# A float32 transformer trunk on one core: another opening, and four seven-product chunks in the last stage

## The chip, the core and the metric

The kernel runs on one core of one Trainium2 chip. The metric is the device time of one execution in microseconds (us). The engines named below: TensorE (PE in the profile; PEld is its weight load), VectorE (DVE), ScalarE (ACT), GpSimd (POOL) and SyncE (SP), which issues most DMAs. Each engine works through its own instructions in program order; an instruction whose operands are not ready holds everything behind it on that engine.

## What is computed

Two layers of a streaming encoder on 256 frames of width 1024, all in float32. Each layer is a half-step SwiGLU network (hidden width 2816), attention (chunked with a relative bias in layer 0, differential with rotary in layer 1, both beside a cross-attention into a memory of 256 rows), and a second half-step SwiGLU network:

```python
for i in range(DEPTH):
    h = rmsnorm(x, ffn1_norm[i])
    x = x + 0.5 * swiglu(h, ffn1_w_gate[i], ffn1_w_up[i], ffn1_w_down[i])
    h = rmsnorm(x, mix_norm[i])
    proj = h @ w_in[i]
    ...
    x = x + jnp.concatenate([o_s, o_m], axis=-1) @ w_out[i]
    h = rmsnorm(x, ffn2_norm[i])
    x = x + 0.5 * swiglu(h, ffn2_w_gate[i], ffn2_w_up[i], ffn2_w_down[i])

def swiglu(h, w_gate, w_up, w_down):
    return (jax.nn.silu(h @ w_gate) * (h @ w_up)) @ w_down
```

The row scale of `rmsnorm` is applied behind the product, so the gate and up products start from x times the gain, before the mean square is known.

## The kernel before

**Split products.** A float32 operand is split into a high part that TensorE's fast float32 mode (`F32R`) holds exactly, and a low part, the rest. A product of a weight tile and an x tile is then three matmuls into one PSUM bank: high times high, low weight times high x, high weight times low x. `dense` (L504) issues them, at L511, L514 and L517. Weights arrive in chunks of 1 MB (128 partitions by 2048 columns, `raw`); ScalarE casts the high parts (`split_hi`, L338), VectorE subtracts the low parts (`split_lo`, L356), both in pieces. Three raw buffers and four pairs of high and low buffers go round. `Item.units` lists the pieces that a chunk is split into.

**Gate and up.** A network has 11 groups of 256 hidden columns. A group's gate and up columns lie side by side, 512 columns. K is 1024, eight tiles of 128, so a group has two chunks, `c` = 0 for K tiles 0 to 3 and `c` = 1 for 4 to 7. For each of the two token blocks (`tb`, 128 frames each) a group accumulates in one PSUM bank; `plain_chunk` (L750) runs `dense` over token blocks and tiles, 24 matmuls for a chunk. `evac` (L624) applies the row scale and the activation behind a group, turns the result (`h`, `hb`) and sends it through DRAM (`hd`, `hr`) to become the operand of the down product. In each network, two of the groups are done as seven products instead of eight (`pair_forms`, `product`); for these VectorE forms four sums of the x tiles (L780) and their splits (`xf`, L784 and L787) as soon as all of x is there.

**Down.** 11 chunks of 256 rows by 1024 columns, each eight products of three matmuls; chunks listed in `SEVEN` take seven products (`seven`, `seven_item`): VectorE forms four sums of the weight tiles (L350, `wsum`), seven pieces are split rather than four, and the operand gets sums of its own (`seven_forms`, L681 and L694). The first chunk of the list takes two buffer pairs; the others are guests: their last pieces lie in the tiles that hold x's split parts at other times (`xt_room`), one guest at a time. Chunks 8 to 10 run at the end, one output quarter after the other (`SPLIT`), and `finish` adds each quarter to x.

**Order.** The program is written out by hand-set rules: a planner (`Flow`) keeps a clock of its own while the code is being generated. PE's work advances it (0.216 us for a matmul); each helper is a thread (a Python generator) that yields the time or the condition at which its next step is due, and steps are put into the engines' programs when the planner's clock reaches them. Threads go ahead of idle threads; the loader and the two splitters are idle threads. A splitter also waits until its engine is nearly free (`calm_a`, `calm_v`), and the pair forms wait for VectorE to be nearly free in the same manner.

**The opening.** `load_x` (L185) loads x in quarters (token block by half of the columns); the first half of each block is issued at the start, on SP's and ScalarE's queues. The loader issues the first chunk in eight pieces, the second in four, with the second half of block 0 behind the first chunk and that of block 1 in the middle of the second. A small array of gains is transposed (L1631); PE runs warm products of the identity, four at the start, then two and five (L1646, called from L1636 and L1638). `start` (L1640) prepares the quarters of x at the planner's times 3.4, 8.8, 5.6 and 10.8: `prep_half` (L547) transposes four tiles on PE (L525), scales them by the gain on VectorE (`y`, L557), casts the high part on ScalarE (`xh`, L560) and subtracts the low part on VectorE (`xl`, L562). Then the first network goes through group 0's two chunks, in halves of two K tiles, for both token blocks.

Of the kernel before, what the change touches and what calls it, by code (L numbers as in the profile page):

```python
# [142 lines left out]
def kernel(  # L143
# [40 lines left out]

    def load_x(tb, hf, queue=None):  # L185
        (queue or nc.sync).dma_start(out=xs[tb][:, hf * 512:(hf + 1) * 512],
                                     in_=x[0, tb * P:(tb + 1) * P, hf * 512:(hf + 1) * 512])

    load_x(0, 0)
    load_x(1, 0, nc.scalar)  # L190

# [55 lines left out]
    class Item:  # L247
# [3 lines left out]
        def __init__(self, raws, uses=8, w=1):  # L251
            self.raws, self.uses = raws, uses
            self.hi = self.lo = None
            self.hit, self.lot, self.st = [None] * 7, [None] * 7, [None] * 4
            self.n, self.frees, self.takes, self.gives, self.guest = 1, 1, 0, 0, False
            self.sums, self.t = [], []
            self.index = len(items)
            w = 1 if len(items) < 2 else w
            self.units = [(self.own(q, w), q, w, None) for q in range(0, 4, w)]
            items.append(self)  # L260
# [13 lines left out]
    xt_room = [False]  # L274
    dma_free = [2.5]
    LAT = 1.5
# [9 lines left out]
    def loader():  # L286
        for i, c in enumerate(chunks):
            yield lambda: raw_left[0] > 0
            raw_left[0] -= 1
            c.raw = wraw.tile([P, 2048], F32, tag="raw", name=f"raw{i}")  # L290
            dma_free[0] = max(dma_free[0], flow.now)
            n = len(c.parts)
            for j, (dst, src) in enumerate(c.parts):
                nc.sync.dma_start(out=dst(c.raw), in_=src)
                dma_free[0] += 2.9 / n
                if i < 2 and j % 2:
                    for q in range((j - 1) * 4 // n, (j + 1) * 4 // n):
                        c.block[q] = dma_free[0] + LAT
                if i == 1 and j == 1:
                    load_x(1, 1)  # L300
                    dma_free[0] += 0.7
            c.arrive = dma_free[0] + LAT
            c.block = [t or c.arrive for t in c.block]
            if i == 0:
                load_x(0, 1)
                dma_free[0] += 0.7
            if i > 4 and late_done[0] < len(late_loads):
                dst, src = late_loads[late_done[0]]
                late_done[0] += 1
                nc.sync.dma_start(out=dst, in_=src)  # L310
                dma_free[0] += 0.3
# [30 lines left out]
    def split_lo():  # L342
        for i, it in enumerate(items):
# [8 lines left out]
            for src, q, w, dep in it.units:  # L352
                yield lambda: it.hit[q] is not None
                yield it.hit[q]
                yield calm_v(i)
                nc.vector.tensor_sub(it.part(1, q, w), src(), it.part(0, q, w).bitcast(F32))  # L356
                t = flow.dve(512 * w)
                it.lot[q:q + w] = [t] * w
            raw_left[0] += it.frees
            g2.give(it.gives)  # L360
# [15 lines left out]

    SEVEN = {(0, 1): (), (0, 2): (1, 4, 7), (1, 1): (1, 4, 7), (1, 2): (1, 4, 7)}
    PAIR = {(0, 1): 4, (0, 2): 3, (1, 1): 3, (1, 2): 3}
# [63 lines left out]
    def plan_ffn(l, nm, wg, wu, wd):  # L442
# [7 lines left out]
        pair = PAIR[l, nm]  # L450
        work = [(g, c) for g in range(NG) for c in range(2)]
        if pair is not None:
            rest = [w for w in work if w[0] not in (pair, pair + 1)]
# [50 lines left out]
    def dense(ps, xh, xl, ready, c, need, start, stop):  # L504
# [17 lines left out]
        return flow.pe(T_MM)  # L522

    def turn(dst, src, flipped=False):
        nc.tensor.transpose(out=dst, in_=src, identity=flip if flipped else ident)  # L525
        return flow.pe(T_TR)
# [9 lines left out]
    class Xt:  # L536
        def __init__(self, keep=False):
# [6 lines left out]
            self.done = [0, 0]  # L544
            self.keep, self.y, self.ft = keep, {}, [None] * 4

    def prep_half(xt, tb, hf, gc, wait=0.0):  # L547
# [10 lines left out]
        banks.give()  # L558
        yield flow.dve(512)
        nc.scalar.copy(out=xt.h[tb][:, ks, :], in_=y)  # L560
        yield flow.act(512)
        nc.vector.tensor_sub(xt.l[tb][:, ks, :], y, xt.h[tb].bitcast(F32)[:, ks, :])  # L562
        if xt.keep:
            xt.y[tb, hf] = y
        else:
            g2.give()
# [51 lines left out]
    def ffn(l, nm, xt, gc_next):  # L618
# [230 lines left out]
        if (l, nm) != (0, 1):  # L849
            for tb in range(2):  # L850
                for c in range(2):
                    plain_chunk(0, c, (tb,))
        else:
            for c in range(2):
                for ks in ((0, 1), (2, 3)):
                    plain_chunk(0, c, range(2), ks)
        work = work[2:]
        for w in work:
# [770 lines left out]
    def start_gain():  # L1629
        tp = bank("gps0")  # L1630
        nc.tensor.transpose(out=tp[:, 0, :16], in_=g1row, identity=ident[:16, :16])  # L1631
        yield flow.pe(T_TR)
        nc.vector.tensor_copy(gcol[:, 0:16], tp[:, 0, :16])
        banks.give()
        flow.dve(16)
        warm(2)  # L1636
        yield 4.6
        warm(5)  # L1638

# [10 lines left out]
    warm(4)  # L1650
    table_hint(AF.Silu)
    flow.now = 2.7
    flow.spawn(start_gain())
    for tb in range(2):
        for hf in range(2):
            flow.spawn(start(tb, hf, (3.4, 8.8, 5.6, 10.8)[2 * tb + hf]))
    flow.spawn(gain_columns())
# [61 lines left out]
```

## Time and profile before

| | |
|---|---|
| Time, median of 3 runs | 954.87 us (954.74 to 955.77) |
| The profiled execution: its own time | 955.69 us |
| Its span, from first to last instruction | 953.9 us |
| DVE busy | 820.0 us (86%) |
| ACT busy | 587.0 us (62%) |
| Bytes moved by DMA | 204.04 MB, 214 GB/s on the mean |
| Share of the chain that ended last: PE, DVE, DMA, ACT | 90%, 6%, 2%, 1% |

A line of the timeline gives the start, the time taken, the engine, the line of the kernel, the operation, output and inputs by name, and the count where several are merged; in brackets, how long the engine had been idle and what ended that. A line of the groups gives busy time, mean of one in ns, and idle time ahead of it. A line of the windows gives, for a stretch, the busy time of PE, PEld, DVE, ACT and POOL, the granted clock, the share of the DMA engines and GB/s.

### The profile page before, as it was taken

What the parts mean: (1) busy time and instruction counts of PE and PEld (TensorE: products, weight loads), DVE (VectorE), ACT (ScalarE), POOL (GpSimd) and SP (SyncE); (2) the same over time, 40 slices, a digit from 0 to 9 for tenths busy, and PEclk for the clock granted to TensorE, in tenths of its full rate; (3) what the DMA queues carried; (4) which work ended last, traced back from release to release, by engine and by line L of the source; (5) the groups of instructions that cost most, each with busy time, mean ns of one, the idle gap of its engine ahead of it and who ended that gap; (6) DMA issues with size and microseconds to landing.
All of it is one profiled execution on the core that took longest, in us unless ns stands there. A gap on an engine that the chain in (4) does not pass through costs nothing.

```text
span 953.9 us, 13334 instructions
## 1 busy us (share of the span) xinstructions
PE 945.6 (99%) x4475; PEld 774.1 (81%) x4475; DVE 820.0 (86%) x1483; ACT 587.0 (62%) x1121; POOL 109.1 (11%) x160
## 2 busy tenths in 40 slices
PE   9999999999999999999999999999999999999998
PEld 7888888887777888888888888888787778888886
DVE  7898978888777899979889899796999888999884
ACT  6556566677676746647546656564676865665650
POOL 1000057621210100000000000000434200000000
PEclk9999999999999999999999999999999999999999
DMA  8987799486525387887746679775641367588751
GB/s 265 289 263 236 224 354 296 158 276 210 177 90 177 97 266 225 262 287 219 245 146 219 208 226 288 247 253 166 196 158 57 121 214 228 183 275 276 239 197 45
DMA packets 169887, 204.04 MB, mean 214 GB/s; under 512 B 10137, under 2 KB 145114, under 8 KB 169818
## 3 DMA queue, kind: packets, MB, share of 16 engines
q1 hardware_dynamic: 169498, 202.78, 66.0%
q8 instruction: 35, 0.57, 0.3%
q10 hardware_dynamic: 320, 0.40, 0.1%
q14 instruction: 34, 0.28, 0.1%
HBM read 188.99 MB, written 14.16 MB: 213 GB/s over the span
## 4 chain that ended last, share of the span: by engine, by line
PE 90%; DVE 6%; DMA 2%; ACT 1%; issue 1%; SPq 0%; ACTq 0%; DVEq 0%
PE gu L517 13%; PE gu L514 13%; PE gu L511 13%; PE acc L511 9%; PE acc L517 9%; PE acc L514 9%; PE pair_m L511 3%; PE pair_m L514 3%; PE pair_m L517 3%; PE pj L517 2%; PE pj L511 2%; PE pj L514 2%; DVE lo L356 2%; PE S L1360 1%; DMA x<-in_x_dram 1%; PE AV L1441 1%
## 5 line engine op out<-in xcount | busy, mean ns | idle before, releaser
L338 ACT CAST hi<-raw 128x512 fp32r<-128x512 f32 (+1 forms) x467 | 336.3, 770 | 172.6 <-DMA raw<-in_ffn_w_up_dram 45.6
L356 DVE TENSOR_TENSOR lo<-raw,hi 128x512 fp32r<-128x512 f32 (+1 forms) x467 | 391.9, 875 | 35.5 <-ACT hi L338 35.4
L514 PE MATMUL gu<-lo,xh 128*128 128x512 f32 x576 | 224.7, 390 | 0.5 <-DVE lo L356 0.5
L517 PE MATMUL gu<-hi,xl 128*128 128x512 f32 x576 | 224.5, 390 | 0.4 <-DVE xl L562 0.4
L511 PE MATMUL gu<-hi,xh 128*128 128x512 f32 x576 | 224.4, 390 | 0.0
L517 PEld LDWEIGHTS gu<-hi,xl 128*128 128x128 f32 x576 | 108.1, 188 | 23.9 <-DVE xl L562 1.7
L514 PEld LDWEIGHTS gu<-lo,xh 128*128 128x128 f32 x576 | 108.1, 188 | 23.5 <-DVE lo L356 1.4
L511 PEld LDWEIGHTS gu<-hi,xh 128*128 128x128 f32 x576 | 108.2, 188 | 22.3
L517 PE MATMUL acc<-hi,ht 128*128 128x512 f32 x280 | 109.5, 391 | 0.0
L511 PE MATMUL acc<-hi,ht 128*128 128x512 f32 x280 | 109.2, 390 | 0.0
L514 PE MATMUL acc<-lo,ht 128*128 128x512 f32 x280 | 109.1, 390 | 0.0
L338 ACT CAST hi<-wsum 128x512 fp32r<-128x512 f32 x82 | 47.7, 619 | 26.5 <-DVE wsum L350 26.5
L514 PE MATMUL pj<-lo,xh 128*128 128x512 f32 x160 | 64.0, 400 | 0.0
L517 PE MATMUL pj<-hi,xl 128*128 128x512 f32 x160 | 63.8, 399 | 0.0
L511 PE MATMUL pj<-hi,xh 128*128 128x512 f32 x160 | 63.8, 399 | 0.0
L514 PEld LDWEIGHTS acc<-lo,ht 128*128 128x128 f32 x280 | 52.6, 188 | 10.9
L517 PEld LDWEIGHTS acc<-hi,ht 128*128 128x128 f32 x280 | 52.6, 188 | 10.8
L511 PEld LDWEIGHTS acc<-hi,ht 128*128 128x128 f32 x280 | 52.6, 188 | 10.7
L532 POOL TENSOR_TENSOR xr<-v,nhalf 128x1 f32<-128x1 f32 x12 | 10.3, 861 | 435.1 <-DVE v L530 435.1
L356 DVE TENSOR_TENSOR lo<-wsum,hi 128x512 fp32r<-128x512 f32 x82 | 52.8, 680 | 0.0
L633 ACT ACTIVATE sil<-gu,xr 128x256 f32<-128x256 f32 x72 | 33.7, 468 | 29.8 <-PE gu L517 29.7
L532 POOL TENSOR_TENSOR hf<-v,nhalf 128x8 f32<-128x8 f32 (+1 forms) x20 | 31.4, 1570 | 87.3 <-DVE v L530 78.9
(232 smaller groups left out, 1429.5 us busy)
## 6 DMA issues: line engine op xcount, KB each, us to landing
raw<-in_ffn_w_down_dram SPq DMA_DIRECT2D x176, 256.0 KB, 4.5
raw<-in_ffn_w_gate_dram SPq DMA_DIRECT2D x82, 512.0 KB, 4.0
raw<-in_ffn_w_up_dram SPq DMA_DIRECT2D x82, 512.0 KB, 5.4
raw<-in_w_in_dram SPq DMA_DIRECT2D x32, 512.0 KB, 4.4
hd<-hb SPq DMA_DIRECT2D x44, 256.0 KB, 4.6
hr<-hd SPq DMA_DIRECT2D x44, 256.0 KB, 4.6
raw<-in_w_out_dram SPq DMA_DIRECT2D x8, 1024.0 KB, 5.1
raw<-in_w_mem_kv_dram SPq DMA_DIRECT2D x4, 1024.0 KB, 5.3
```

What stands on the lines that cost most here:

```text
L338: nc.scalar.copy(out=it.part(0, q, w), in_=src())
L356: nc.vector.tensor_sub(it.part(1, q, w), src(), it.part(0, q, w).bitcast(F32))
L511: nc.tensor.matmul(out=ps, lhsT=xh, rhs=wh, start=start, stop=False)
L514: nc.tensor.matmul(out=ps, lhsT=xh, rhs=wl, start=False, stop=False)
L517: nc.tensor.matmul(out=ps, lhsT=xl, rhs=wh, start=False, stop=stop)
L532: nc.gpsimd.tensor_tensor(out=dst, in0=v[:, :n], in1=nhalf[:, :n], op=ALU.pow)
L633: nc.scalar.activation(sil, ps[tb][:, 0:256], AF.Silu, scale=xt.r[tb])
L1360: nc.tensor.matmul(out=ss[e][:, pr, :nk], lhsT=q[rows, pr, :], rhs=k[rows, pr, :], start=i == 0, stop=i == len(passes) - 1)
L1441: nc.tensor.matmul(out=av[64 * e:64 * e + 64, pr, :], lhsT=vsrc(kb, pr, e), rhs=pts[e][:, pr, kb, :], start=(kb == 0), stop=(kb == nb - 1))
```

## The change

Four things are changed.

1. x comes in other pieces. Block 0's first half is loaded in two pieces on two queues; block 1's first half is issued behind the first two weight pieces; the second halves come behind the second chunk. Three of the first chunk's eight pieces go through ScalarE's queue, and the load of the activation table stands behind the first of them.
2. The first network begins with the first halves of K of groups 0 and 1, then their second halves: chunks (0,0), (1,0), (0,1), (1,1).
3. K tiles 0 and 1 of the first chunk are not split: each is multiplied as a plain float32 product of raw weights and scaled x (`whole`), four products for two tiles and two token blocks. The first raw buffer is given back when these are done. The last seven warm products go.
4. In the last network, chunks 1, 3, 5 and 7 of the down product take seven products, in place of 1, 4 and 7.

```diff
-    def load_x(tb, hf, queue=None):
-        (queue or nc.sync).dma_start(out=xs[tb][:, hf * 512:(hf + 1) * 512],
-                                     in_=x[0, tb * P:(tb + 1) * P, hf * 512:(hf + 1) * 512])
-
-    load_x(0, 0)
-    load_x(1, 0, nc.scalar)
+    def load_x(tb, hf, q=0, n=2, queue=None):
+        sl = slice(hf * 512 + q * 256, hf * 512 + (q + n) * 256)
+        (queue or nc.sync).dma_start(out=xs[tb][:, sl], in_=x[0, tb * P:(tb + 1) * P, sl])
+
+    load_x(0, 0, 0, 1)
+    load_x(0, 0, 1, 1, nc.scalar)
...
-            self.units = [(self.own(q, w), q, w, None) for q in range(0, 4, w)]
+            whole = 0 if items else 2
+            self.units = [(self.own(q, w), q, w, None) for q in range(whole, 4, w)]
...
-    dma_free = [2.5]
+    dma_free = [2.95]
...
+            lat = LAT if i > 1 else 0.6
             for j, (dst, src) in enumerate(c.parts):
-                nc.sync.dma_start(out=dst(c.raw), in_=src)
-                dma_free[0] += 2.9 / n
+                (nc.scalar if i == 0 and j in (1, 6, 7) else nc.sync).dma_start(out=dst(c.raw), in_=src)
+                dma_free[0] += 3.0 / n
                 if i < 2 and j % 2:
                     for q in range((j - 1) * 4 // n, (j + 1) * 4 // n):
-                        c.block[q] = dma_free[0] + LAT
-                if i == 1 and j == 1:
-                    load_x(1, 1)
-                    dma_free[0] += 0.7
-            c.arrive = dma_free[0] + LAT
+                        c.block[q] = dma_free[0] + lat
+                if i == 0 and j == 1:
+                    table_hint(AF.Silu)
+                    load_x(1, 0)
+                    dma_free[0] += 0.75
+            c.arrive = dma_free[0] + lat
             c.block = [t or c.arrive for t in c.block]
-            if i == 0:
-                load_x(0, 1)
-                dma_free[0] += 0.7
+            if i == 1:
+                for tb in range(2):
+                    load_x(tb, 1)
+                    dma_free[0] += 0.75
...
+            if i == 0:
+                yield lambda: whole_left[0] == 0
             raw_left[0] += it.frees
...
-    SEVEN = {(0, 1): (), (0, 2): (1, 4, 7), (1, 1): (1, 4, 7), (1, 2): (1, 4, 7)}
+    SEVEN = {(0, 1): (), (0, 2): (1, 4, 7), (1, 1): (1, 4, 7), (1, 2): (1, 3, 5, 7)}
...
+        if (l, nm) == (0, 1):
+            work[:4] = [(g, c) for c in range(2) for g in range(2)]
...
+    whole_left = [4]
+
+    def whole(ps, xt, tb, c, k):
+
+        flow.until(lambda: tb in xt.first)
+        y, t = xt.first[tb]
+        flow.at(max(t, c.raws[0].block[k] + 0.2))
+        nc.tensor.matmul(out=ps, lhsT=y[:, k, :], rhs=c.own(k)(), start=k == 0, stop=False)
+        c.uses -= 1
+        whole_left[0] -= 1
+        if k == 1 and not xt.keep:
+            g2.give()
+        for _ in range(4):
+            flow.pe(T_MM)
+            flow.step()
...
-            for c in range(2):
-                for ks in ((0, 1), (2, 3)):
-                    plain_chunk(0, c, range(2), ks)
-        work = work[2:]
+            open_[0] = [bank(f"gu{tb}", (P, 512)) for tb in range(2)], [None, None]
+            flow.spawn(evac(0, *open_[0]))
+            for k in range(2):
+                for tb in range(2):
+                    whole(open_[0][0][tb], xt, tb, plan[l, nm, "gu"][0, 0], k)
+            plain_chunk(0, 0, range(2), (2, 3))
+            work = work[1:]
...
-        warm(2)
-        yield 4.6
-        warm(5)
...
     warm(4)
-    table_hint(AF.Silu)
     flow.now = 2.7
...
-            flow.spawn(start(tb, hf, (3.4, 8.8, 5.6, 10.8)[2 * tb + hf]))
+            flow.spawn(start(tb, hf, (3.4, 12.0, 4.6, 13.0)[2 * tb + hf]))
```

In `prep_half` the scaled x (`y`) of the two first halves and the time at which it is due are kept in `xt.first` for `whole`.

More of the change, by code (lines that the diff above doesn't have):

```diff
@@ L544, in __init__ @@
             self.done = [0, 0]
-            self.keep, self.y, self.ft = keep, {}, [None] * 4
+            self.keep, self.y, self.ft, self.first = keep, {}, [None] * 4, {}
     def prep_half(xt, tb, hf, gc, wait=0.0):
@@ L558, in prep_half @@
         banks.give()
-        yield flow.dve(512)
+        t = flow.dve(512)
+        opening = gc == GC_FFN1 and hf == 0
+        if opening:
+            xt.first[tb] = y, t
+        yield t
         nc.scalar.copy(out=xt.h[tb][:, ks, :], in_=y)
@@ L564, in prep_half @@
             xt.y[tb, hf] = y
-        else:
+        elif not opening:
             g2.give()
@@ L852, in ffn @@
                     plain_chunk(0, c, (tb,))
+            work = work[2:]
         else:
-            for c in range(2):
-                for ks in ((0, 1), (2, 3)):
-                    plain_chunk(0, c, range(2), ks)
-        work = work[2:]
+            open_[0] = [bank(f"gu{tb}", (P, 512)) for tb in range(2)], [None, None]
[5 more added lines that the diff above has]
+            work = work[1:]
         for w in work:
```

## The prediction, made before the changed kernel was seen

> **What bounds the kernel now.** I read the page's busy times first, then the chain of waits, then the timeline of the first 30 us and of the last stage, and the windows and groups of that stage.
>
> ```profile
> PE 945.6 (99%) x4475; PEld 774.1 (81%) x4475; DVE 820.0 (86%) x1483; ACT 587.0 (62%) x1121; POOL 109.1 (11%) x160
> ```
>
> PE (TensorE) is busy in 945.6 of 953.9 us. So there are two ways to shorten this program: fewer matmuls where PE runs without a break, or less waiting in the few places where it doesn't. The end of the program is of the first kind:
>
> ```profile
> 913.79 0.39 PE L517 MATMUL m<-hi,h 128*128 128x512 f32 x1
> ...
> 918.55 0.39 PE L517 MATMUL acc<-hi,ht 128*128 128x512 f32 x1
> ```
>
> Between these two starts lie the seven products of one seven-product chunk, 21 matmuls: (918.55 - 913.79) / 21 = 0.2267 us is the pitch of a matmul. The opening is of the second kind (timeline, PE, then the chain of waits):
>
> ```profile
> 1.35 2.08 PE L1646 MATMUL warm<-ident 128*128 128x128 f32 x8 [1.35 <-POOL ident masks.py:199]
> ...
> 3.58 1.22 PE L1646 MATMUL warm<-ident 128*128 128x128 f32 x4
> 4.59 1.06 PE L525 MATMUL xtp<-ident,x 128*128 128x128 f32 x4
> 5.44 1.49 PE L1646 MATMUL warm<-ident 128*128 128x128 f32 x10
> 6.77 0.60 PE L525 MATMUL xtp<-ident,x 128*128 128x128 f32 x4
> 7.13 0.48 PE L511 MATMUL gu<-hi,xh 128*128 128x512 f32 x1
> ...
> 12.93 0.40 PE L517 MATMUL gu<-hi,xl 128*128 128x512 f32 x1
> ```
> ```profile
> 1.18 3.89 DMA x<-in_x_dram
> ...
> 6.93 5.22 DMA x<-in_x_dram
> ...
> 12.20 0.66 PE xtp L525 x4
> 12.86 0.23 PE gu L514
> ...
> 23.11 0.34 PE gu L514
> ...
> 28.68 0.28 PE gu L514
> ```
>
> The twelve matmuls of K tiles 0 and 1 (two token blocks, two tiles, three matmuls each) run from 7.13 to 12.93 + 0.23 = 13.16 us, 5.8 us of waiting on loads and splits for 2.7 us of work. From there each matmul takes its 0.23; the pieces of 0.34 and 0.28 show that PE is just met by the splits of the third and fourth chunk: a lead there is worth something only if those splits come earlier too. They hang on this stretch of VectorE (DVE):
>
> ```profile
> 13.38 0.68 DVE L557 TENSOR_TENSOR y<-xtp,gcol 128x512 f32<-128x512 f32 x1
> ...
> 16.04 0.68 DVE L562 TENSOR_TENSOR xl<-y,xh 128x512 fp32r<-128x512 f32 x1
> 16.76 2.15 DVE L780 TENSOR_TENSOR y<-y 128x512 f32<-128x512 f32 x3
> ...
> 19.08 0.68 DVE L780 TENSOR_TENSOR y<-y 128x512 f32<-128x512 f32 x1
> 19.68 1.22 DVE L356 TENSOR_TENSOR lo<-raw,hi 128x1024 fp32r<-128x1024 f32 x1
> ...
> 21.07 0.68 DVE L787 TENSOR_TENSOR xf<-y,xf 128x512 fp32r<-128x512 f32 x1
> 21.67 1.22 DVE L356 TENSOR_TENSOR lo<-raw,hi 128x1024 fp32r<-128x1024 f32 x1
> ```
>
> The last quarter of x (token block 1, second half) gets its low part at 16.04; then come the four sums of the pair forms, then the low parts of the third chunk, done at 20.90 (tiles 0 and 1) and 22.89 (2 and 3). The second is what made PE wait at 23.11.
>
> **Part 1, a fourth seven-product chunk.** Chunks 1, 3, 5, 7 in place of 1, 4, 7 leave out one product of eight: 3 x 0.2267 = 0.68 us, if the extra vector work is hidden. The groups, windows and timeline of that stage:
>
> ```profile
> L356 DVE TENSOR_TENSOR lo<-wsum,hi 128x512 fp32r<-128x512 f32 x6 | 4.0, 678 | 0.0
> ...
> L350 DVE TENSOR_TENSOR wsum<-raw,wsum 128x512 f32<-128x512 f32 x4 | 2.8, 688 | 0.1
> ...
> L667 DVE TENSOR_TENSOR ht<-hr,ht 128x512 fp32r<-128x512 f32 x4 | 2.7, 686 | 3.7 <-ACT ht L665 3.7
> ...
> L694 DVE TENSOR_TENSOR h<-sf,h 128x512 fp32r<-128x512 f32 x1 | 0.7, 684 | 0.0
> ...
> L681 DVE TENSOR_TENSOR sf<-hr 128x128 f32<-128x128 f32 x2 | 0.6, 283 | 0.0
> L694 DVE TENSOR_TENSOR h<-hr,h 128x256 fp32r<-128x256 f32 x1 | 0.4, 419 | 0.0
> ...
> L694 DVE TENSOR_TENSOR h<-hr,h 128x128 fp32r<-128x128 f32 x1 | 0.3, 284 | 0.0
> ```
> ```profile
> sum 50.00, PE 50.00 PEld 41.40 DVE 42.34 ACT 30.83 POOL 0.00; mean PE 10.00 PEld 8.28 DVE 8.47 ACT 6.17 POOL 0.00
> ```
> ```profile
> 920.19 1.89 DVE L356 TENSOR_TENSOR gxl<-wsum,gxh 128x512 fp32r<-128x512 f32 x3
> ...
> 931.93 0.39 PE L514 MATMUL m<-gxl,h 128*128 128x512 f32 x1
> ```
>
> One more such chunk costs DVE four sums (4 x 0.69), three more low parts (3 x 0.68), four small sums (4 x 0.28) and 1.4 for three form parts in place of one of 0.69: 6.6 us at most. From 884 to 934 us DVE is idle for 50 - 42.3 = 7.7. The low parts of chunk 7 stand ready at 920.19 + 1.89 = 922.08 and are read from 931.93 on, 9.9 us later. But a seven-product chunk that borrows the x tiles (a "guest") may be split only after the guest before it has been used up; from chunk 4 to 7 that left two chunks of PE time, from 3 to 5 and 5 to 7 it leaves one plain chunk, 24 x 0.2267 = 5.4 us. Passes back to back start (1.89 - 0.68) / 2 = 0.605 apart, so a seven-product and a plain chunk together ask of DVE 15 x 0.605 plus 1.1, 1.4 and 0.7 for the forms, 12.3 at most, in 45 x 0.2267 = 10.2 us of PE: 2.1 short per pair, over two pairs. Against that stands a lead of 9.9 less one chunk, about 4.5 us, so I take the whole 0.68. Bounds: nothing gained, or all of it and no more.
>
> **Part 2, four float32 products.** A float32 product with 512 columns isn't in this trace; the nearest rows are the 128-column ones. A float32 product is recorded as two instructions (the five warm products at 5.44 are ten rows). For the transposes, their tile's row and one window:
>
> ```profile
> L525 PE MATMUL xtp<-ident,x x48: 270/272/421, 4.6 to 320.1; 128*128 128x128 f32 x48
> ```
> ```profile
> 4.00:5.00 1.00, 1.00 (x6) 1.00 (x6) 0.00 (x0) 0.00 (x0) 0.00 (x0) 1.00 1.07 366
> ```
>
> Four of them in 0.60 us (at 6.77) with 0.27 for the last give 0.11 per instruction of 128 columns, so 2 x 4 x 0.11 = 0.88 us per product. The same four at 4.59 take 1.06 with 0.42 for the last: 0.213 each, which would be 1.7 us. PE's clock rises in between, at about 5.9 within the warm products; the column of the granted clock (1.00 at 4 to 5 us) doesn't show it, the durations do. I take 0.88 and keep 1.7 for a rival. [...]
>
> So 12 matmuls (2.72 us) become 4 products (3.5 us): 0.8 us more PE work, in exchange for four splits that are no longer waited for.
>
> **Part 3, the loads and the order.** x block 0 (two pieces on two queues) is needed by the same time as now. x block 1, first half, is issued behind the first two weight pieces. Now it lands at 1.18 + 3.89 = 5.07; by the time the first up piece is in (the split at 5.51 waited for it),
>
> ```profile
> 5.51 0.62 ACT L338 CAST hi<-raw 128x512 fp32r<-128x512 f32 x1 [2.36 <-DMA raw<-in_ffn_w_up_dram]
> ```
>
> 768 KB and the gains are in, as many as will then be ahead of and in that piece of x:
>
> ```profile
> raw<-in_ffn_w_gate_dram SPq DMA_DIRECT2D x4, 128.0 KB
> ...
> x<-in_x_dram ACTq DMA_DIRECT2D x1, 256.0 KB, 3.9
> ```
>
> (two pieces of x at 256, two of weights at 128.) So I take 5.4, with 5.07 and 5.9 for bounds. Its transposes stand in PE's program ahead of the first float32 product. They take 0.44 to 0.85: product 1 starts at 6.1. Product 2 needs block 1's scaled x, one DVE pass of 0.68 after the transposes, 7.0. Four at 0.88 end at 9.65. The splits of tiles 2 and 3 and of x are done by then (four 0.62 casts and four 0.68 subtractions from 5.5 on, between the two scalings). The 12 matmuls of tiles 2 and 3 end at **T1 = 9.65 + 2.72 = 12.4**. Then comes the second group's first half (24 matmuls). The table load and the last two weight pieces on ACT's queue lie before 5 us and hold nothing up; SP's queue gets shorter by four issues, which is cover for the chunks behind.
>
> Now what is late next. By the due times written in the code (12.0 and 13.0) the last two x quarters are transposed inside those 24 matmuls, about after the third and the sixth. Thus the last quarter reaches DVE at T1 + 6 x 0.2267 + 0.44 + 0.60 = T1 + 2.4; scaling (0.68), cast (0.62) and hops bring its low part to T1 + 3.85. In the planner's order the four sums come ahead of the third chunk's low parts, as now (a waiting stage thread goes before the idle splitters). From that low part to the two ends it takes now 20.90 - 16.04 = 4.86 and 22.89 - 16.04 = 6.85, so T1 + 8.7 and **T1 + 10.7 = 23.1**. PE arrives at T1 + 24 x 0.2267 + 0.88 = T1 + 6.3 = 18.7 and stands for over 2 us. Its lead of 2.6 us (13.16 less the 0.88 of transposes still to do, less 9.65) is taken back by DVE: 23.1 in place of 23.05, where PE goes on today. The opening gives 0.1 us away; with T1 anywhere from 11.8 to 13.1 it lies between -0.5 and +0.8. Beyond this point the same work follows, with the first group's gate and up evacuations pushed behind the splits, which helps the fourth chunk by the 0.05 of the 28.68 piece, no more.
>
> Sum: -0.68 + 0.1 = -0.6 us. The profiled execution took 955.69 (span 953.9), 955.1 after the change; it lies 0.8 above the median of the runs shown, so on that scale 954.87 - 0.6 = **954.3**.
>
> **The rivals.** *Slow clock* (the other side): the warm matmuls at 3.58 and 5.44 go, and in their place PE has eight transposes and two pauses. If the clock then rises late, the products cost 1.7 instead of 0.88. Today it rises 4.5 us after the first matmul (1.35 to 5.9); if the pause before 5.4 makes PE earn it anew from there, it rises at 9.9: 3.6 us slow from 6.3, 2.1 products, then 1.9 x 0.88, end 11.6, T1 = 14.3, the chunk at T1 + 10.7 = 25.0: 1.95 lost, 1.3 in all, 956.1. Never in the four products: end 13.1, T1 = 15.9, 957.8. It decides slower against faster from T1 = 13.0 on, that is from one slow product. For it: PE ran 4.5 us at the low clock though it was busy from 1.35 on. Against it: 2.1 us of warm products and a transpose group still stand ahead of the only pause. [...]
>
> *DVE doesn't hold it*: if the third chunk's low parts stand ahead of the sums, PE keeps its 2.6: 954.87 - 2.6 - 0.7 = 951.6. Against: the order now. *The seven-product chunk shows*: DVE late for chunk 5 or 7 by a cast and a subtraction or two, 0.7 to 1.5 us, 955.0 to 955.8.
>
> **How the numbers follow.** Forecast 0.52 (953.7 to 955.0); clock late 0.22 (near 956.1); clock very late 0.09 (957 and over); DVE not holding 0.11; the last stage exposed 0.06. Leaving out the two ends, range 952.4 to 956.9. A change under 0.2% (1.9 us) can't be told from none here: faster than that is the case of DVE not holding, with the tail of the forecast, 0.12; slower the very late clock and part of the late one, 0.12; the rest 0.76.
>
> **What would show it.** Right: the float32 products of 0.44 us per instruction ending near 9.7; a PE idle of 2 us near 19 that ends on the low part of the third chunk; its second pair near 23; 3 matmuls fewer in the last stage and no idle there. Wrong: instructions of 0.85 in the products; PE running through 19 us; PE idle after 900.

## The result, and the profile after

| | before | after |
|---|---|---|
| Time, median of 4 runs | 954.99 us (954.74 to 955.77) | 971.15 us (970.82 to 972.2) |
| Ratio | | 1.0166, 95% interval 1.0151 to 1.0182 |
| The profiled execution: time, span | 955.69, 953.9 us | 972.2, 970.4 us |

The kernel became 1.7% slower; 954.3 us had been forecast, with 956.9 as the upper end. The page of after has PE busy for longer, with fewer instructions:

```profile
PE 950.1 (98%) x4454; PEld 774.6 (80%) x4454; DVE 825.1 (85%) x1494; ACT 588.5 (61%) x1124; POOL 109.8 (11%) x160
```

PE has 21 instructions fewer on record than before and is busy for 4.5 us more, so some of them ran slowly; the other 12.0 of the 16.5 us of span are idle time. To find the places, the starts of the same matmuls were compared in the two timelines ("lag": after less before). The first matmul of the first network's pair forms (54.23 us before) lags by 9.64 us. The lag is still 9.64 at the 37th of these matmuls and 17.16 at the 49th (87.29 before). From there to the last network it moves to 17.5 and back to 16.70, and the last network takes 0.68 off; the last matmul lags by 16.02. **So there are two places: the opening, 9.64 us, and something near 90 us, 7.5 us.**

**The opening.** The chain of waits of after, first 17 us (start, time, what):

```profile
1.18 4.24 DMA x<-in_x_dram
5.43 3.30 DMA raw<-in_ffn_w_gate_dram
...
8.76 7.43 DMA raw<-in_ffn_w_up_dram
...
16.27 0.63 ACT hi L342
```

Three DMAs stand one behind the other, and the middle one belongs to another chunk than the last. The timeline of ScalarE (ACT, and ACTq for what it issues) says how:

```profile
1.18 0.44 ACTq L187 DMA_DIRECT2D x<-in_x_dram  x1
1.65 0.45 ACTq L296 DMA_DIRECT2D raw<-in_ffn_w_up_dram  x1
...
3.43 0.20 ACT L941 ACTIVATE dummy<-dummy 128x1 f32<-128x1 f32 x1
7.86 0.35 ACTq L296 DMA_DIRECT2D raw<-in_ffn_w_gate_dram  x1
8.76 0.33 ACTq L296 DMA_DIRECT2D raw<-in_ffn_w_up_dram  x1
9.13 1.14 ACT L588 CAST xh<-y 128x512 fp32r<-128x512 f32 x2 [5.50 <-DMA raw<-in_ffn_w_gate_dram]
10.18 0.61 ACT L342 CAST hi<-raw 128x512 fp32r<-128x512 f32 x1
16.27 1.14 ACT L342 CAST hi<-raw 128x512 fp32r<-128x512 f32 x2 [5.48 <-DMA raw<-in_ffn_w_up_dram]
```

The last two weight pieces of the first chunk are issued at 7.86 and 8.76, not before 5. Each follows the landing of an earlier DMA by 0.02 to 0.03 us (8.73 ends the 3.30 us of the chain). In the trace's records the issues of the two pieces wait for semaphores 101 and 102, on which the DMAs issued at 3.54 and 5.43 signal their end (landing at 7.84 and 8.73). On ScalarE this wait stands in the program ahead of the casts: the first cast, whose input VectorE wrote from 6.19 to 6.88, runs at 9.13, and the two pieces land at 14.4 and 16.19 us, behind the megabyte of the second chunk that SP had issued from 5.43 on. PE stands until the cast of tile 3 (PE's timeline, then windows of 3.4 us; the column behind POOL is the granted clock, and ahead of the first rise, at 8.76, it shows 1.00 where the first two instructions of the float32 products start 0.85 us apart, against 0.43 behind it):

```profile
7.29 4.33 PE L539 MATMUL gu<-raw,y 128*128 128x512 f32 x8
...
12.07 0.40 PE L525 MATMUL gu<-hi,xl 128*128 128x512 f32 x1
16.94 0.80 PE L519 MATMUL gu<-hi,xh 128*128 128x512 f32 x1 [4.47 <-ACT hi L342]
```
```profile
12.20:15.60 3.40, 0.27 (x2) 0.00 (x0) 0.00 (x0) 0.00 (x0) 0.00 (x0) 1.00 1.03 358
15.60:19.00 3.40, 2.06 (x4) 1.44 (x5) 1.72 (x3) 2.73 (x7) 0.00 (x0) 0.50 0.27 64
19.00:22.40 3.40, 3.40 (x9) 2.59 (x9) 1.56 (x3) 1.20 (x4) 0.00 (x0) 0.50 0.95 307
```

The idle of 4.5 us is paid for twice: behind it the granted clock is 0.50 for 6.8 us (15.59 to 22.41), about 8 matmuls in 3.40 us in place of 15.

**The second place.** SP's timeline, then PE's:

```profile
93.85 0.37 SPq L314 DMA_DIRECT2D grow<-in_b_subln_dram  x1
```
```profile
93.72 0.40 PE L522 MATMUL gu<-lo,xh 128*128 128x512 f32 x1
98.57 0.32 PE L231 MATMUL gps<-ident,grow 55*128 55x55 f32 x1 [4.46 <-DMA hd<-hb]
98.83 0.79 PE L525 MATMUL gu<-hi,xl 128*128 128x512 f32 x1
```

The rows of all later gains (`grow`) come as small loads behind one chunk each; when the last is due, a small transpose on PE reads them. In after PE reaches this transpose as the last row is being issued and stands 4.5 us. (The view names `hd<-hb`, the DMA issued next, as the one that landed last; the operand is `grow`.) Again 6.8 us at half clock (97.51 to 104.33) follow, with matmuls of 0.63 in place of 0.39. Before, the transpose ran at 83.79, 5.5 us behind the same load:

```profile
78.29 0.36 SPq L310 DMA_DIRECT2D grow<-in_b_subln_dram  x1
```

A kernel that waits there starts the transpose 3.6 to 4.7 us behind the issue (after, e1, e5, e7, e8, e12, e13), so the margin before was 0.8 to 1.9 us; and SP is 15.6 us later in after where PE is 9.6 us later. What SP waits for between 20 and 94 us shows a difference, before, then after (us, times, longest):

```profile
SPq L656 <- DMA hd<-hb: 1.5, 1, 1.5
```
```profile
SPq L684 <- DMA hd<-hb: 8.8, 3, 4.5
```

`hr` reads back what `hd` wrote to DRAM. In after SP reaches the read too early and stands, and eight weight pieces stand behind it:

```profile
62.58 0.64 SPq L678 DMA_DIRECT2D hd<-hb  x1
67.80 0.37 SPq L684 DMA_DIRECT2D hr<-hd  x1
68.31 0.42 SPq L296 DMA_DIRECT2D raw<-in_ffn_w_gate_dram  x1
```

Before, the same eight pieces were issued between the write and the read. The planner had put the steps in another order, because a few of its times had moved.

**The last stage** went as forecast. The 50 us that answer to the window shown of before:

```profile
899.00:949.00 50.00, 50.00 (x222) 41.42 (x221) 47.90 (x93) 33.11 (x66) 0.00 (x0) 1.00 0.59 191
```

VectorE has 5.6 us more to do and PE still runs without a break.

### The profile page after: what moved, and what is told of

Its sections match the earlier page's. It is cut to its first block, busy times and chain, and to the rows that moved or that the text cites. A ratio compares the mean times of both kernels' runs of the same rounds, so it can differ in the third digit from the quotient of the medians.

```text
span 970.4 us, 13296 instructions
## 1 busy us (share of the span) xinstructions
PE 950.1 (98%) x4454; PEld 774.6 (80%) x4454; DVE 825.1 (85%) x1494; ACT 588.5 (61%) x1124; POOL 109.8 (11%) x160
## 4 chain that ended last, share of the span: by engine, by line
PE 83%; DVE 7%; DMA 6%; ACT 2%; SPq 1%; issue 1%; ACTq 0%; DVEq 0%
PE gu L525 11%; PE gu L519 11%; PE gu L522 11%; PE acc L519 9%; PE acc L525 8%; PE acc L522 8%; DMA raw<-in_ffn_w_up_dram 3%; DVE lo L360 3%; PE pj L525 2%; PE pj L522 2%; PE pj L519 2%; PE pair_m L522 2%; PE pair_m L519 2%; PE pair_m L525 2%; SPq L296 1%; PE S L1392 1%
## 5 line engine op out<-in xcount | busy, mean ns | idle before, releaser
L525 PE MATMUL acc<-hi,ht 128*128 128x512 f32 x272 | 106.4, 391 | 0.0
L519 PE MATMUL acc<-hi,ht 128*128 128x512 f32 x272 | 106.1, 390 | 0.0
L522 PE MATMUL acc<-lo,ht 128*128 128x512 f32 x272 | 106.0, 390 | 0.0
L519 PEld LDWEIGHTS acc<-hi,ht 128*128 128x128 f32 x272 | 51.1, 188 | 10.4
L525 PEld LDWEIGHTS acc<-hi,ht 128*128 128x128 f32 x272 | 51.1, 188 | 10.4
L588 ACT CAST xh<-y 128x512 fp32r<-128x512 f32 x24 | 14.8, 619 | 46.9 <-DVE y L581 41.4
```

Source lines behind the costliest of these rows:

```text
L519: nc.tensor.matmul(out=ps, lhsT=xh, rhs=wh, start=start, stop=False)
L522: nc.tensor.matmul(out=ps, lhsT=xh, rhs=wl, start=False, stop=False)
L525: nc.tensor.matmul(out=ps, lhsT=xl, rhs=wh, start=False, stop=stop)
```

## The experiments

Theory: ScalarE's wait in front of the two pieces makes the idle, the idle makes the half clock, and SP's late row of gains is a stall of its own kind. Rivals: the float32 products or the new order of chunks cost the time; the two stalls have one cause. Ratios are to the kernel before on the same chip; lags and clocks are of one profiled execution each, which can lie off the median: e8's is the fastest of its runs (954.83 us, median 958.09), e13's the second fastest (955.59, median 957.83), e7's the slowest (963.88, median 961.57). "Clock rises at" is the trace's first record of the granted clock. How far one execution can be off shows in e8 and e9: their PE and VectorE work through the same instructions in the same order up to 85 us, yet the lag at the first pair form is -2.13 in one and -1.01 in the other.

| | clock rises at | lag, first pair form | behind the gains | end of first network | last matmul | median us | ratio, 95% |
|---|---|---|---|---|---|---|---|
| after | 8.76 | 9.64 | 17.16 | 17.2 | 16.02 | 971.15 | 1.0166 (1.0151 to 1.0182) |
| e1 | 10.49 | 3.44 | 9.49 | 9.50 | 7.37 | 963.62 | 1.0076 (1.0051 to 1.0101) |
| e2 | 9.75 | 9.35 | (9.05) | 12.08 | 11.32 | 968.51 | 1.0125 (1.0097 to 1.0152) |
| e3 | 5.53 | 0.12 | 0.12 | 0.12 | -0.08 | 954.86 | 0.9988 (0.9976 to 1.0) |
| e4 | 9.33 | 6.49 | 14.05 | 14.15 | 12.15 | 969.44 | 1.0137 (1.0112 to 1.0161) |
| e5 | 4.80 | 1.09 | 6.95 | 6.97 | 6.13 | 962.79 | 1.0073 (1.0058 to 1.0088) |
| e6 | 8.34 | -0.90 | -0.74 | 1.27 | 1.72 | 958.14 | 1.0034 (1.0019 to 1.0049) |
| e7 | 10.43 | 3.31 | 9.17 | 9.20 | 8.09 | 961.57 | 1.0061 (1.0040 to 1.0082) |
| e8 | 6.02 | -2.13 | 0.11 | 0.11 | -0.95 | 958.09 | 1.0025 (1.0014 to 1.0035) |
| e9 | 6.41 | -1.01 | (-0.65) | 0.99 | 0.52 | 957.25 | 1.0012 (1.0000 to 1.0024) |
| e10 | 13.38 | 0.88 | (0.46) | 1.07 | 1.23 | 955.77 | 0.9998 (0.9986 to 1.0011) |
| e11 | 4.95 | 0.85 | (0.43) | 1.75 | -0.13 | 957.36 | 1.0012 (1.0003 to 1.0022) |
| e12 | 10.26 | 3.23 | 3.70 | 3.71 | 1.77 | 958.61 | 1.0032 (1.0020 to 1.0044) |
| e13 | 5.34 | -0.77 | 0.64 | 1.58 | -0.08 | 957.83 | 1.0021 (1.0010 to 1.0033) |
| e14 | 7.47 | -0.75 | (-1.17) | 0.85 | 0.74 | 956.89 | 1.0019 (1.0007 to 1.0032) |

"Behind the gains" is at the 49th matmul of the pair forms; in brackets where the transpose of the gains comes later than that. "End of first network" is at the transposes behind it, 177.73 us before.

**e1: the two pieces on SP's queue.**

```diff
-                (nc.scalar if i == 0 and j in (1, 6, 7) else nc.sync).dma_start(out=dst(c.raw), in_=src)
+                (nc.scalar if i == 0 and j == 1 else nc.sync).dma_start(out=dst(c.raw), in_=src)
```

> The last two weight pieces of the first chunk go through SP's queue again. Theory (ScalarE stood behind DMA issues that wait for a free DMA semaphore): the pieces are issued near 5.4 and 5.9 us in place of 7.86 and 8.76 and land by 9.5 in place of 14.4 and 16.2; PE's idle of 4.5 us behind tile 2 goes, and with it the 6.8 us of half clock behind it. PE then stands about 2 us for the second halves of x, which land a microsecond later than now. Lag against the kernel before at the first pair product: +1 to +3 us in place of +9.64. If the second stall, at the transpose of the gains near 94 us, hangs on this lag: 955 to 958 us. Rival 1, the second stall has a cause of its own: 962 to 965. Rival 2, the float32 products and the new order of groups cost the time: 966 or more.

The idle behind tile 2 is gone and 6.2 us of the 9.64 with it. So the queue of two DMAs was worth most of the opening's loss. The second stall stayed (4.4 us of idle): the two have not one cause, and rival 1 named the time. PE's timeline of e1 shows what is left of the opening:

```profile
6.50 5.58 PE L539 MATMUL gu<-raw,y 128*128 128x512 f32 x8
11.52 0.79 PE L519 MATMUL gu<-hi,xh 128*128 128x512 f32 x1
...
21.05 0.39 PE L519 MATMUL gu<-hi,xh 128*128 128x512 f32 x1
23.30 0.50 PE L522 MATMUL gu<-lo,xh 128*128 128x512 f32 x1 [1.86 <-DVE lo L360]
```

Eight instructions of four float32 products take 5.4 us where the clock rises at 10.49, and PE stands 2 us for the third chunk's low part, as it does in the forecast. VectorE's timeline has the reason in the order that the forecast named, four sums and then the low part:

```profile
19.24 2.87 DVE L808 TENSOR_TENSOR y<-y 128x512 f32<-128x512 f32 x4
22.03 1.22 DVE L360 TENSOR_TENSOR lo<-raw,hi 128x1024 fp32r<-128x1024 f32 x1
```

**e2: the transposes of late small loads 20 us behind their last load** (after, `flow.now + 8.0` made 20.0 in `loaded`).

> The transposes of the late small loads stand 20 us behind the last of their loads in the planner's time, in place of 8. Theory (PE stands 4.6 us for the last row of gains, issued by SP at 93.85, and runs 6.8 us at half clock behind it): the second stall goes, the lag stays near +9.6 at the last pair products and 963 to 964.5 us come out. Rival (the second stall is an ordinary wait for weights that comes out at another place): 970 to 972.

The stall at the gains went, but 2.6 us were lost again around two waits for low parts at 119.9 and 125.3 us. VectorE had stood 3.7 us up to 110.7, behind a late read of hidden values (`hr`), and was then busy for 11.96 of 12 us (114 to 126). That this comes from SP's queue, as late as before, is argued. 968.51 lies between the two cases.

**e3: the seven-product chunks alone** (before, with `(1, 2): (1, 3, 5, 7)`).

> The kernel before with chunks 1, 3, 5 and 7 as seven products in the last network, and nothing else of the change. Theory (hidden vector work, three matmuls fewer): -0.68 us, 954.2 to 954.4 us by the median of before. Rival (vector work shows in the last stage): 954.9 to 955.8.

```profile
883.00:933.00 50.00, 50.00 (x223) 41.40 (x222) 47.85 (x93) 33.12 (x65) 0.00 (x0) 1.00 0.59 191
```

PE has no gap, and the lag falls from 0.56 ahead of the last network to -0.08: 0.64 us, as the theory says. The ratio, 0.12% under 1 with an interval that touches 1, fits it and could not show it alone.

**e4: 20 warm products in the idle behind tile 2** (after, otherwise unchanged).

```diff
-            plain_chunk(0, 0, range(2), (2, 3))
+            plain_chunk(0, 0, (0,), (2,))
+            warm(20)
+            plain_chunk(0, 0, (0,), (3,))
+            plain_chunk(0, 0, (1,), (2, 3))
```

> The changed kernel with 20 warm products of the identity (two instructions of 0.11 us each, 4.4 us) put into PE's idle between tiles 2 and 3 of the first chunk; all loads and waits as in the changed kernel. Theory (the half clock from 15.6 to 22.4 us is the price of the idle itself, a second cost of about 3.4 us on top of the 4.5): the wait for tile 3 ends at the same 16.9 us, the clock stays at 1.0, the lag at the first pair product falls from +9.64 to about +6.2, time about 967.5 us. Rival (the half clock is set by something else, the load of the engines or the float32 products): lag and time stay, 970.5 to 972.

```profile
12.10 4.62 PE L1678 MATMUL warm<-ident 128*128 128x128 f32 x40
16.48 0.48 PE L519 MATMUL gu<-hi,xh 128*128 128x512 f32 x1
```
```profile
12.20:15.60 3.40, 3.40 (x33) 3.40 (x32) 0.01 (x1) 0.66 (x2) 0.00 (x0) 1.00 0.91 303
```

Tile 3 comes nearly as late as in after (16.48), but PE has work, the clock stays at 1.00, and the lag falls by 3.15 us (3.4 expected). The half clock was the price of the idle itself here. The profile bears the theory out; the time, 2 us over the 967.5 named, has the second stall in full (+7.56).

**e5: e1, with a warm product in each of PE's two pauses among the transposes.**

```diff
+            if gc == GC_FFN1 and hf == 0 and (tb, k) in ((0, 2), (1, 0)):
+                warm(1)
             t = turn(tp[:, k, :], xs[tb][:, hf * 512 + k * P:hf * 512 + (k + 1) * P])
```

> The kernel with all late pieces on SP's queue (e1), and one warm product of the identity in each of PE's two pauses among the transposes of the first halves of x. In e1 the clock rose only at 10.49 us and the first float32 products took 0.85 us an instruction. Theory (the removed warm products kept PE busy enough for the clock to rise near 6 us, and their loss is about 2 us of the opening): the clock rises before 7.5 us, the products end near 10.2 in place of 12.1, the third chunk's matmuls go on near 21.4 in place of 23.3; lag at the first pair product 0 to +1.7 in place of +3.44, time 960 to 962 us with the second stall still there. Rival (the clock rises on a timer of its own, whatever PE does): lag +3 to +5, time 963 to 965.

```profile
6.24 3.79 PE L539 MATMUL gu<-raw,y 128*128 128x512 f32 x8
```

The clock rises at 4.80, the products take 0.43 us an instruction from the start, the lag is 1.09. In the seven kernels of the changed opening without these warm products the clock rises between 8.3 and 10.5 us; in the six with them that keep the float32 products, between 4.8 and 7.5. So here it hangs on what PE does, as the theory says. The 2.35 us are not all of that: 1.5 are there at the third chunk's low part (23.30 in e1, 21.84 in e5), the rest comes behind it, where e1 ran 3.4 us at half clock and e5 did not. The stall of the gains was untouched, so the time is above what was expected.

**e6: e1, with VectorE's four sums behind the fourth chunk's low parts.**

```diff
             yield lambda: len(xt.y) == 4 and g4.left >= 4
+            if (l, nm) == (0, 1):
+                yield lambda: items[3].lot[3] is not None
```

> e1, and VectorE's four sums of the pair forms wait until the low parts of the fourth chunk are written. Theory (as in the prediction: the sums ahead of the third chunk's low parts make PE stand 2 us near 21.3 us, and the half clock behind it is its second price): PE runs through, no half clock behind it, lag at the first pair product near -0.3 in place of +3.44. SP's order of loads moves with it, so the second stall may stay (time 959 to 961 us) or go (953.5 to 955). Rival (the third chunk's weights come too late in any case): lag stays above +2.

PE does not stand at 21 us and the lag is -0.90: the sums in front of the low parts were what made it stand. With the sums SP's order moved, and the last row of gains was in time (issued at 81.5). But from the first pair form to 307 us the kernel loses 4.2 us, of which 2.6 are idle in three waits of PE for VectorE (at 113, 179 and 235 us); 958.14 lies between the two times that were named.

**e7: e1, with the reads of the hidden values 2 us later in the first network** (`flow.now + 2.0` made 4.0).

> e1, and the loads that read a group's turned hidden values back from DRAM stand 4 us behind the release of their buffer in the planner's time, in place of 2, in the first network only; by that two chunks of weights stand ahead of such a load in SP's queue again, as in the kernel before. Theory (SP stands for the write to DRAM with eight weight pieces queued behind it, so the last row of gains is issued a chunk late): it is issued near 81.5 us in place of 87.3, the stall of 4.5 us at the transpose of the gains and its half clock go, the lag of +3.4 stays to the end: 957 to 958.5 us. Rival (the raw buffers come free late, whatever the order): the stall stays, 962 to 965.

```profile
84.71 0.36 SPq L314 DMA_DIRECT2D grow<-in_b_subln_dram  x1
```

SP no longer waits for any write to DRAM, yet the row is issued only 2.6 us earlier than in e1 (87.32), while PE comes 1.1 us earlier too; 2.9 us of the stall stay. The theory missed here in the profiled run, the slowest of five (958.56 to 963.88). From 55 us on, VectorE's and ScalarE's steps stand in another order than in e1, so the run says little on the reads alone.

**e12: e1, with those reads on GpSimd's queue instead**, the same order on PE, VectorE and ScalarE.

```diff
-            nc.sync.dma_start(out=hr, in_=hd.rearrange("a i b x -> (i b) a x"))
+            (nc.gpsimd if (l, nm) == (0, 1) else nc.sync).dma_start(out=hr, in_=hd.rearrange("a i b x -> (i b) a x"))
```

> e1, and the loads that read the turned hidden values back go through GpSimd's queue in the first network; the order on PE, VectorE and ScalarE is e1's, and SP has nothing left that waits for a write to DRAM (8.8 us in three waits between 20 and 94 us in e1). Theory (these waits make SP late): the last row of gains is issued at 79 to 82 us in place of 87.3, PE's stall of 4.5 us at the transpose of the gains goes with its half clock, the lag of about +3.4 stays to the end of the network: 957 to 958.5 us. Rival (SP hangs on VectorE's splits, which give the raw buffers back): issued at 84.5 or later, a stall of 3 us or more stays, 960 to 964.

```profile
L314 SPq DMA_DIRECT2D grow<-in_b_subln_dram x1: 365/365/365, 83.5 to 83.5; - x1
```

The row comes 3.8 us earlier, less than expected, but PE now stands only 0.4 us there, the clock stays up, and the lag of 3.23 goes on as 3.71. So SP's waits for the writes to DRAM made most of the second stall. They are not all that makes the row late: it is issued 5.2 us later than in the kernel before (78.29), with PE 3.2 us later; what the other 2 us come from is not shown.

**e8 to e11, e13 and e14: can the changed opening win?** e8 is e5, e6 and e7 together. e9 is e8 with the transpose of the gains alone 20 us behind its last load. e10 is e9 with tiles 0 and 1 of the first chunk split as before (no float32 products). e11 is e9 with both halves of group 0 first. e13 is e5, e6 and e12 together; e14 is e13 with the later transpose.

> e5, e6 and e7 together: warm products in the pauses, sums behind the fourth chunk's low parts, hidden values read back 2 us later. Theory: float32 products done near 10.2 us, no idle of PE over 1 us before 130 us, no half clock; lag at the first pair product -2.6 to -1.5, held to the last stage, where 0.68 more goes: 951.5 to 953 us. Rival (a lead of PE is used up by the next chunks' splits): lag -0.5 to +0.5, 954 to 955.

> e8 (-2.13 us against the kernel before at the first pair product, of which 2.24 were lost again at the transpose of the gains), and the transpose of the gains alone stands 20 us behind its last load in the planner's time, in place of 8. Theory (the row of gains comes by SP's queue, whose time hangs on VectorE's splits and not on PE, so a lead of PE runs into it): the stall of 2.35 us goes, the lead of 2.1 is held through the network and 0.7 comes in the last stage: 2.8 us under the kernel before on the same chip, ratio 0.997, about 952 on the scale of 955. Rival (the same lateness comes out at the next weights, as in e2 near 120 us): 1.5 to 2.5 us are lost at another place before 130 us, ratio 0.999 to 1.000.

> e9 with K tiles 0 and 1 of the first chunk split again (three matmuls for each tile and block, no float32 products). Theory (the float32 products take four splits out of the way of the first matmuls): the first matmuls wait for casts and subtractions, T1 comes 1 to 2.5 us later than in e9, the lag at the first pair product is -1 to +0.5 in place of about -2.1. Rival (0.88 us for a product against 0.68 for three matmuls gives the gain back): lag within 0.3 us of e9's.

> e9 with the order of chunks of the kernel before: both halves of K of group 0, then group 1. Loads of x as in the changed kernel, the second halves behind the second chunk. Theory (two first halves ahead give the second halves of x 24 matmuls of time): PE stands for x's second halves from 12.9 us to about 16.5 and the lag at the first pair product is +1 to +3 in place of about -2.1. Rival (the order matters little, since VectorE's chain sets the time of the third chunk): within 0.5 us of e9.

> e5 and e6 (warm products in the pauses, sums behind the fourth chunk's low parts) with the reads of the hidden values on GpSimd's queue as in e12, at their old times. Theory (SP's waits took the lead of e8): the last row of gains is issued by 80 us, no stall over 0.5 us there, lag -2 at the first pair product and -1.5 or less at the end of the first network, ratio 0.997 to 0.998. Rival (VectorE's splits bound the first network): the lead is down to between -0.5 and +1.5 by 130 us, ratio 0.999 to 1.001.

> e13 with the transpose of the gains 20 us behind its last load in the planner's time, in place of 8. Theory (SP's waits took the lead): as e13 or 0.3 us better. Rival (VectorE's splits): lag between -0.5 and +1.5 by 130 us as well, ratio 0.999 to 1.001.

In e8 the opening at last has its lead, 2.13 us; it is lost where it meets the row of gains. e9 has no stall there, and loses its lead around waits for low parts (0.5 us at 81, 0.35 at 113 among them). In e10 and e11 the lag at the first pair form is 1.9 us more than in e9 (0.88 and 0.85 against -1.01). So the float32 products and the new order of chunks are each worth something there. The size is uncertain, since e8, e9, e13 and e14, with one opening, lie between -2.13 and -0.75; in e10 part of it is the clock, which rose only at 13.38, and for e11 its theory had wanted 3 us or more. The times do not show that worth: e10, without the float32 products, has 955.77 us against 957.25 in e9. At the end of the first network all six lie between 0.1 and 1.8 us behind the kernel before. e13 and e14 have no waits of SP for writes to DRAM, and end no better, so the theory that these waits took the lead is wrong. In e13 the row of gains is late all the same (issued at 83.39, not by 80): PE stands 1.4 us there, and then 0.6 us at 115 for a low part. e14, without the stall, loses its lead around a wait of 0.7 us for a low part at 112. The rival, VectorE's work, is nearer, but it does not account for e13's stall, and the ratios lie above its 0.999 to 1.001. VectorE's busy time from 4 to 24 us (third number behind the comma), before and e13:

```profile
4.00:24.00 20.00, 19.04 (x90) 14.65 (x90) 17.17 (x30) 15.27 (x29) 1.86 (x2) 1.00 0.89 289
```
```profile
4.00:24.00 20.00, 19.82 (x84) 14.06 (x83) 14.17 (x22) 13.17 (x24) 1.54 (x2) 1.00 1.00 317
```

PE did more in e13 and VectorE 3.0 us less, which it would have to make up in a stretch where it is about 90% busy. By 115 us it has not: from 24 us on it is busy for 79.9 of 91 us in e13 and for 82.3 before. That this work is what takes the lead is argued from these figures and the names of the waits, not shown by a run of its own.

No variant of the opening beats the kernel before. The seven-product chunk alone (e3) has the lowest ratio seen, with an interval that touches 1.

## Why the prediction was wrong

**The step that failed**, as the prediction put it: "The table load and the last two weight pieces on ACT's queue lie before 5 us and hold nothing up; SP's queue gets shorter by four issues". They were issued at 7.86 and 8.76 us, each behind the landing of an earlier DMA, and held up every cast of the opening. That alone is 6.2 of the 9.64 us (e1), 3.15 of them the half clock behind the idle (e4). The profile before had a hint, in SP's timeline of the first 6 us:

```profile
4.02 0.48 SPq L294 DMA_DIRECT2D raw<-in_ffn_w_gate_dram  x1
5.09 0.33 SPq L294 DMA_DIRECT2D raw<-in_ffn_w_up_dram  x1
```

SP issues a piece every 0.47 us and then stands for 0.6 us, although the buffer is there from the start; the piece at 5.09 waits in the trace for semaphore 102, on which x block 1 signals its end, and x block 1 landed at 5.07 (1.18 + 3.89 in the chain of before).

**A second step failed by saying nothing**: "Beyond this point the same work follows". The work is the same, but the order in SP's queue isn't, and 7.5 us came from a row of 512 bytes whose margin before was 0.8 to 1.9 us. In e1's kernel this place costs 6.05 us (3.44 to 9.49), and with the reads off SP's queue 0.5 (e12).

**The clock.** The rival was right that the clock rises late, with the wrong time: it rose at 8.76 in after (9.9 in the rival) and at 8.3 to 10.5 in every kernel of this opening without warm products in the pauses; putting them back was worth 2.35 us (e1 to e5), the half clock behind e1's idle included. What no case contained was a second fall of the clock: in after it went to 0.50 for 6.8 us behind each of the two idles of 4.5 us, which made of the one at the gains a loss of about 7.5. (The sum for the clock that never rises is 0.1 too high: 13.1 + 2.72 is 15.8, not 15.9.)

**What held.** The float32 product: 0.43 us an instruction behind the rise at 8.76 in after (0.44 forecast), 0.85 ahead of it. VectorE's chain: PE stands 2 us for the third chunk's low part when the stalls are taken out (e1, e5), and taking the sums out of its way frees it (e6). The last stage: -0.64 in e3 and -0.68 in after (-0.68 forecast), with VectorE's extra work hidden, 5.6 us against at most 6.6. x block 1 landed at 5.55 in e1 (5.4 taken). What the forecast did not ask is when block 0's second piece lands: at 5.42 in after (1.18 + 4.24 in the chain), so its transposes resume only at 5.46. Where neither ScalarE's wait nor the late clock is left (e5, the forecast's own case), the lag is 1.09 and not 0.1: T1 is 12.6 (12.4 forecast), and the third chunk's second pair comes at 24.1 (T1 + 11.5, forecast T1 + 10.7).

**No variant kept a gain of the opening.** The forecast thought that a lead of the opening would be taken back by one chain near 23 us. In e8, e9, e13 and e14 a lead survives this and is lost later in the first network, at the row of gains or around waits for low parts.

## What to carry to other kernels

A DMA issued from a computing engine is an instruction in that engine's order: ask what it can wait for at issue (a free semaphore, a buffer), and what stands behind it (in after the first cast ran at 9.13, 2.25 us behind the end of its input). When a change moves the times by which an order is written out, compare the order on every queue, not only on the engine that bounds; a small load with a margin of 1 to 2 us is where it shows. Price an idle of PE with the clock behind it: 4.5 us of idle were followed by 6.8 us at half clock in after, 1.9 us by 3.4 in e1, and 1.9 us by none in e5.

## What the runs showed of the hardware

**The granted clock.** In the records of after it is 1.00 from 8.76 us, 0.50 from 15.59 to 22.41, 1.00 up to 97.51 and 0.50 up to 104.33; each of the two stretches of 6.83 us at half clock goes with an idle of PE of 4.5 us (12.47 to 16.94, 94.11 to 98.57). In after the clock stayed up behind an idle of 1.9 us that ended at 30.42, in this stretch (first number behind the comma: PE busy; ends of matmuls are modelled),

```profile
29.24:32.66 3.42, 1.66 (x6) 1.05 (x6) 3.35 (x8) 3.42 (x6) 1.95 (x2) 1.00 0.00 0
```

and in e1, behind an idle of the same 1.9 us in the first of these two stretches, the second ran at half clock:

```profile
20.73:24.15 3.42, 1.56 (x8) 0.96 (x7) 3.35 (x7) 3.42 (x8) 0.56 (x1) 1.00 0.25 83
24.15:27.56 3.41, 3.40 (x9) 2.21 (x8) 3.38 (x6) 2.37 (x4) 1.75 (x2) 0.50 0.21 38
```

In e5 PE stood for 1.9 us as well and was busy for 1.53 of 3.41 us from 18.45 to 21.86, and the clock stayed at 1.00; so what made the difference is not shown. Ahead of the first rise PE was busy for 3.07 of 3.41 us in after (5.35 to 8.76), and in e10, where the clock rose at 13.38, for 2.97 of 3.42 us from 6.55 to 9.97 and for all of 3.41 us from 9.97 on. The times of e1 go with the mean clock: its runs at 0.998, 0.996 and 0.994 took 961.85, 963.6 and 966.39 us.

Of the 3.07 us ahead of the rise in after, 1.80 were float32 transposes, which the trace records as matmuls (the same stretch, instructions of the transposes' tile alone):

```profile
5.35:8.76 3.41, 1.80 (x6) 1.00 (x6) 1.38 (x2) 1.00 0.89 273
```

What the transposes alone do for the rise no run shows.
